# Gated feed-forward up-projection: seven-product pairs raised from 8 to 14 per layer, weight sums formed by adding transfers in memory

## The chip, the cores and the metric

The kernel runs on one core of a Trainium2 chip. The metric is the device time of one execution in microseconds; a run's time is the median over repeated executions. The profile shown here is of one execution on the same core. The engines are called PE (TensorE, with PEld for its weight loads), DVE (VectorE), ACT (ScalarE), POOL (GpSimd) and SP (SyncE, which here only issues transfers).

## The reference

The kernel computes a two-layer decoder trunk on 512 tokens of width 1024, all in float32. Each layer has an attention mixer and then a gated feed-forward block with a causal convolution of width 3 along the tokens. Only the feed-forward block matters here:

```python
def causal_dwconv(h, w, b):          # w: (3, channels), one filter per channel
    y = lax.conv_general_dilated(h, w[:, None, :], (1,), [(CONV_WIDTH - 1, 0)], ...,
                                 feature_group_count=c)
    return y + b

def conv_ffn(h, w_up, conv_w, conv_b, w_down):      # h: (1, 512, 1024)
    u = causal_dwconv(h @ w_up, conv_w, conv_b)     # w_up: (1024, 5632)
    gate, up = jnp.split(u, 2, axis=-1)             # 2816 each
    return (jax.nn.silu(gate) * up) @ w_down        # w_down: (2816, 1024)

for i in range(DEPTH):                              # DEPTH = 2
    ...                                             # mixer, residual
    h = conv_ffn(rms_norm(x, ffn_pre_g[i]), ffn_w_up[i], ffn_conv_w[i], ffn_conv_b[i], ffn_w_down[i])
    x = x + rms_norm(h, ffn_post_g[i])
```

## The kernel before, in words

**Numbers in two parts.** Every float32 operand of a large product is split into a high and a low part (`split`, `Weights.split`: ACT rounds the high part, DVE subtracts it from the value). A product is three matmuls, high by high, high by low and low by high (`mm3`, lines 290 to 292). A weight *unit* is a 128x1024 float32 block: SP loads it into one of three buffers `wraw` (line 52 or 144), ACT makes `wh` (line 74), DVE makes `wl` (line 75). The class `Weights` keeps a list of units, in the order of use, and prepares some of them ahead of the product that uses them.

**The up-projection.** 2816 gate and 2816 up features are 22 blocks of 128 each. A *pair* is one gate block and the up block that multiplies it; there are 22 pairs, indexed by `n`. The input is held transposed, features of the model on the partitions (8 blocks `k` of 128) and the 512 tokens along the row. An ordinary pair takes 2 (gate, up) x 8 (`k`) x 3 = 48 matmuls of 512 tokens. After it, ACT scales the sum out of PSUM (line 509), DVE adds the two shifted taps (lines 510 and 512), ACT applies silu (line 514), and DVE multiplies gate by up. After each second pair DVE also forms four sums and differences of token blocks (lines 529 to 532) and splits one block of results (`split`, line 199), because the down-projection is done with seven products too.

**Seven products.** For the pairs in `SEVEN` (8 of 22) the product is seen as two by two blocks: gate or up, by the lower or upper half of `k`, by the lower or upper half of the tokens. Seven block products take the place of eight (Strassen's scheme in Winograd's form). One block product is 4 (`k`) x 3 = 12 matmuls of 256 tokens, so a pair takes 84 of these. Four of the seven use sums of input blocks (`x_sums`, made once per layer), and four use sums of weight blocks. In the kernel before, the weight sums are made by `up_sums`: it loads the same two units that an ordinary pair loads and lets DVE do four 128x512 additions or subtractions (lines 150, 151, 154 and 157) on the raw blocks before the split. A seven-product pair has 3.5 units to split (three of 1024 columns and one of 512), an ordinary pair two. Between the products ACT copies two 256-wide partial results (lines 468 and 472) and DVE adds one of them to PSUM twice (lines 475 and 479).

**What sets the order.** In the up-projection of the kernel before, a planner that knows the instructions' estimated costs sets the order on each engine; it may mix the matmuls of an ordinary pair among those of a seven-product pair. In other stages the order is written out by hand (`manual_schedule`). Each engine's queue runs strictly in its order, whoever set it. SP's queue holds nearly all loads. POOL's queue holds small 128x1 operations: the reciprocal roots of the norms in attention (up to 36 us and again from 140 us in layer 0) and at the end of each feed-forward block; in between it is empty.

Of the kernel before, what the change touches and what calls it, by code (L numbers as in the profile page):

```python
# [17 lines left out]
P = 128  # L18
# [18 lines left out]
SEVEN = (4, 6, 8, 10, 12, 14, 16, 18)  # L37


class Weights:  # L40
# [8 lines left out]
    def load(self):  # L49
        src, w = self.units[len(self.raws)]  # L50
        raw = self.raw_pool.tile([P, 1024], F32, tag="wraw", name="wraw", bufs=3)
        self.nc.sync.dma_start(raw[:, :w], src)
        self.raws.append(raw)
# [35 lines left out]
def trunk(tc, A, out):  # L89
# [3 lines left out]
    with ExitStack() as top:  # L93
# [40 lines left out]
        def up_sums(src):  # L134


            raws = []
            lo, hi = slice(0, S), slice(S, 2 * S)

            def unit(n):  # L140
                if n == 0:
                    for z in range(2):
                        raws.append(wpool.tile([P, 1024], F32, tag="wraw", name="wraw", bufs=3))
                        nc.sync.dma_start(raws[z][:], src[z])
                a, b = raws
                h, l = W.pair()
                if n == 0:
                    W.split(h, l, a, 1024)
                elif n == 1:
                    DVE.tensor_tensor(a[:, lo], a[:, lo], b[:, lo], ALU.subtract)  # L150
                    DVE.tensor_tensor(b[:, lo], b[:, lo], b[:, hi], ALU.add)
                    W.split(h, l, b, 1024)
                elif n == 2:
                    DVE.tensor_tensor(b[:, hi], b[:, hi], a[:, lo], ALU.subtract)
                    W.split(h, l, b[:, hi], S)
                else:
                    DVE.tensor_tensor(a[:, hi], a[:, hi], b[:, hi], ALU.subtract)
                    W.split(h, l, a, 1024)
                return h, l

            return [lambda n=n: unit(n) for n in range(4)]

        def ffn_units(layer):
            up = []
            for f in range(NF):
                if f in SEVEN:
                    up += up_sums(A["ffn_w_up"][layer, f])
                else:
                    up += [(A["ffn_w_up"][layer, f, z], 1024) for z in range(2)]
# [203 lines left out]
        def ffn(layer, xnT, pending, final):  # L373
            with ExitStack() as es:
# [3 lines left out]
                nc.sync.dma_start(cw[:], A["ffn_conv"][layer])  # L378
                g_tile = lambda: (fp.tile([P, 1024], F32R, tag="gh", name="gh", bufs=HF),
# [50 lines left out]
                def x_sums():  # L430
# [12 lines left out]

                    def parts(n, x):
# [3 lines left out]
                    return ([lambda: whole_block(a, 0, 0), lambda: whole_block(b, 0, 256), lambda: sub(a, b, a)]  # L448
                            + parts(0, a)
                            + [lambda: whole_block(c, 4, 256), lambda: sub(b, c, b)] + parts(2, b)  # L450
                            + [lambda: sub(c, c, a)] + parts(1, c)
                            + [lambda: whole_block(d, 4, 0), lambda: sub(d, d, c)] + parts(3, d))

                steps = None

                def seven(u, p5):

                    z1, z2 = u[0][:, :256], u[0][:, 256:]
                    c21, c22 = u[1][:, :256], u[1][:, 256:]
                    def product(o, w, half, x, fresh):  # L460
                        for k in range(4):
                            b = slice(half * S + k * P, half * S + (k + 1) * P)
                            xs = [v[:, k] if isinstance(x, list) else v[:, k * 256:(k + 1) * 256] for v in x]
                            mm3(o, w[0][:, b], w[1][:, b], *xs, fresh and k == 0, k == 3, not fresh)

                    wa = W.next()
                    product(c21, wa, 0, x_block(0, 0), True)
                    ACT.copy(z1, c21)
                    wb = W.next()
                    p = bank("t", "p5")[:, :256]  # L470
                    product(p, wb, 0, sums[0], True)
                    ACT.copy(p5, p)
                    wc = W.next()
                    product(c21, wc, 0, sums[1], False)
                    DVE.tensor_tensor(z2, c21, p5, ALU.add)  # L475
                    product(z1, wa, 1, x_block(4, 0), False)
                    wd = W.next()
                    product(c21, wd, 0, sums[2], False)
                    DVE.tensor_tensor(c22, c21, p5, ALU.add)
                    product(z2, wd, 1, x_block(4, 256), False)  # L480
                    product(c21, wb, 1, sums[3], False)

                y1 = None
                for n, f in enumerate(PAIRED):
                    if 3 <= n < min(SEVEN):
                        steps = x_sums() if n == 3 else steps
                        for _ in range(16 if n < min(SEVEN) - 1 else len(steps)):
                            if steps:
                                steps.pop(0)()
                    both = [bank(t, "u") for t in "sa"] if n in SEVEN else None  # L490
                    y = sp.tile([P, 2, S], F32, tag="y", name="y")
# [3 lines left out]
                    if both:  # L495
                        seven(both, y[:, 1, :256])
                    for z in range(2):
                        if n < 2:
                            u = u4[2 * n + z]
                        elif both:  # L500
                            u = both[z]
                        else:
# [233 lines left out]
        def even():  # L736
            with ExitStack() as es:
# [51 lines left out]
                with ExitStack() as e1:  # L789
# [116 lines left out]
                    with ExitStack() as e2:  # L906
# [41 lines left out]
                        for z in range(2):  # L948
                            diff_qk(0, z)
# [840 lines left out]
```

## Time and profile before

| | |
|---|---|
| median of 3 runs | 1136.51 us (1136.33 to 1136.59) |
| profiled execution, its own time | 1136.53 us |
| its span in the trace | 1134.7 us |
| PE busy | 1123.8 us (99%), 6216 matmul records |
| DVE busy | 902.9 us (80%) |
| ACT busy | 614.4 us (54%) |
| POOL busy | 58.2 us (5%) |
| transfers | 126.43 MB, mean 111 GB/s |
| granted PE clock | 0.999 |

The up-projection's matmuls run from 233.8 us to 471.9 us in layer 0 and from 785 us to 1023.5 us in layer 1. The profile's page gives the busy time of each engine and the chain of work that ended last; the views behind it group instructions by line and shape, list them in order of time, say who waited for whom, and give busy time, transfer share and transfer rate for any stretch of the span. A duration in the trace includes some overlap with the next instruction on the same engine, so the distance between two starts is often the better price.

### The profile page before, as it was taken

How to read it: one execution, taken by the hardware profiler on the slowest of the kernel's cores; microseconds unless marked ns; L12 is line 12 of the kernel's file. 1: busy time of each engine (PE TensorE's matmuls, PEld its weight loads, DVE VectorE, ACT ScalarE, POOL GpSimd, SP SyncE). 2: the span in 40 equal slices, each digit the busy share in tenths (PEclk: the TensorE clock that was granted, in tenths of full speed). 3: DMA queues.
4: the chain of work that ended last, by engine and by line, in shares of the span. 5: the costliest groups of instructions: out<-in, count | busy, mean ns of one | idle time of the engine just before them, and what ended most of it. 6: DMA issues, size and time to landing. Idle time of an engine off the chain costs nothing.

```text
span 1134.7 us, 16492 instructions
## 1 busy us (share of the span) xinstructions
PE 1123.8 (99%) x6216; PEld 943.7 (83%) x6216; DVE 902.9 (80%) x1539; ACT 614.4 (54%) x1042; POOL 58.2 (5%) x139
## 2 busy tenths in 40 slices
PE   9999999999999999999999999999999999999997
PEld 8876777898988988887888877888989988988886
DVE  6677576489998998898974476677998998889896
ACT  5465576346555554556643454564455555455562
POOL 2100011210000000000030000002000000000002
PEclk9999999999999999999999999999999999999999
DMA  7310421141423424345736213222123323334461
GB/s 296 112 65 1 137 94 50 44 145 48 144 77 103 119 77 139 107 153 165 228 107 187 88 56 93 77 76 112 59 75 115 109 79 119 101 119 150 146 207 75
DMA packets 39632, 126.43 MB, mean 111 GB/s; under 512 B 5760, under 2 KB 6912, under 8 KB 39424
## 3 DMA queue, kind: packets, MB, share of 16 engines
q1 hardware_dynamic: 37632, 121.63, 33.5%
q10 hardware_dynamic: 1920, 3.74, 1.1%
q8 instruction: 49, 0.80, 0.3%
q14 instruction: 31, 0.25, 0.1%
HBM read 117.98 MB, written 6.32 MB: 110 GB/s over the span
## 4 chain that ended last, share of the span: by engine, by line
PE 89%; DVE 5%; DMA 2%; ACT 2%; issue 2%; POOL 0%; SPq 0%; POOLq 0%; DVEq 0%; ACTq 0%
PE u L290 13%; PE u L292 13%; PE u L291 13%; PE acc L290 4%; PE acc L292 4%; PE acc L291 4%; PE apt L290 3%; PE apt L291 3%; PE apt L292 2%; PE ao L290 2%; PE ao L292 2%; PE ao L291 2%; DVE wl L75 2%; PE sps L984 2%; PE aqk L290 1%
## 5 line engine op out<-in xcount | busy, mean ns | idle before, releaser
L74 ACT CAST wh<-wraw 128x1024 fp32r<-128x1024 f32 (+1 forms) x230 | 232.8, 1019 | 167.0 <-PE u L291 59.2
L75 DVE TENSOR_TENSOR wl<-wraw,wh 128x1024 fp32r<-128x1024 f32 (+1 forms) x230 | 270.4, 1183 | 59.5 <-ACT wh L74 58.9
L290 PE MATMUL u<-xh,wh 128*128 128x512 f32 (+1 forms) x704 | 240.8, 343 | 0.0
L291 PE MATMUL u<-xl,wh 128*128 128x512 f32 (+1 forms) x704 | 240.0, 341 | 0.0
L292 PE MATMUL u<-xh,wl 128*128 128x512 f32 (+1 forms) x704 | 239.5, 341 | 0.0
L290 PEld LDWEIGHTS u<-xh,wh 128*128 128x128 f32 x704 | 133.4, 189 | 17.9 <-DVE u L475 2.6
L291 PEld LDWEIGHTS u<-xl,wh 128*128 128x128 f32 x704 | 133.5, 190 | 14.6
L292 PEld LDWEIGHTS u<-xh,wl 128*128 128x128 f32 x704 | 133.1, 189 | 14.4
L509 ACT ACTIVATE y<-u,cw 128x512 f32<-128x512 f32 x88 | 67.6, 778 | 56.2 <-PE u L292 49.1
L290 PE MATMUL acc<-wh,gh 128*128 128x512 f32 (+1 forms) x250 | 97.0, 388 | 0.8 <-DVE uu L573 0.8
L291 PE MATMUL acc<-wl,gh 128*128 128x512 f32 (+1 forms) x250 | 96.9, 388 | 0.0
L292 PE MATMUL acc<-wh,gl 128*128 128x512 f32 (+1 forms) x250 | 96.9, 387 | 0.0
L510 DVE SCALAR_TENSOR_TENSOR y<-u,cw,y 128x511 f32<-128x511 f32 x88 | 65.0, 744 | 3.1 <-ACT y L509 2.9
L512 DVE SCALAR_TENSOR_TENSOR y<-u,cw,y 128x510 f32<-128x510 f32 x88 | 65.0, 743 | 0.8
L205 POOL TENSOR_TENSOR rv<-ms,epst 128x1 f32<-128x1 f32 x39 | 12.1, 310 | 896.1 <-ACT junk L257 504.6
L290 PEld LDWEIGHTS acc<-wh,gh 128*128 128x128 f32 x250 | 46.9, 188 | 11.0 <-DVE uu L573 1.4
L292 PEld LDWEIGHTS acc<-wh,gl 128*128 128x128 f32 x250 | 46.9, 188 | 9.6
L290 PE MATMUL u<-gh,wh 128*128 128x256 f32 x192 | 54.7, 285 | 0.1
L291 PEld LDWEIGHTS acc<-wl,gh 128*128 128x128 f32 x250 | 47.0, 188 | 9.5
L292 PE MATMUL u<-gh,wl 128*128 128x256 f32 x192 | 54.3, 283 | 0.0
L291 PE MATMUL u<-gl,wh 128*128 128x256 f32 x192 | 54.3, 283 | 0.0
L290 PE MATMUL apt<-xh,wh 128*128 128x512 f32 x128 | 50.6, 395 | 0.0
(360 smaller groups left out, 2317.0 us busy)
## 6 DMA issues: line engine op xcount, KB each, us to landing
wraw<-in_ffn_w_up SPq DMA_DIRECT2D x88, 512.0 KB, 3.7
wraw<-in_ffn_w_down SPq DMA_DIRECT2D x44, 512.0 KB, 3.6
wraw<-in_od_w_dqk SPq DMA_DIRECT2D x12, 512.0 KB, 3.8
wraw<-in_ffn_w_down SPq DMA_DIRECT2D x22, 256.0 KB, 2.9
wraw<-in_ev_w_dqk SPq DMA_DIRECT2D x8, 512.0 KB, 4.5
wraw<-in_ev_w_out SPq DMA_DIRECT2D x8, 512.0 KB, 3.5
spill<-X SPq DMA_DIRECT2D x8, 512.0 KB, 2.6
X<-spill SPq DMA_DIRECT2D x8, 512.0 KB, 6.1
```

The source lines that it names most:

```text
L74: self.nc.scalar.copy(h[:, :w], raw[:, :w])
L75: self.nc.vector.tensor_tensor(l[:, :w], raw[:, :w], h[:, :w].bitcast(F32), ALU.subtract)
L205: POOL.tensor_tensor(v[:, :n], ms, epst[:, :n], ALU.add)
L290: PE.matmul(o, lh, rh, start=first, stop=False, skip_group_check=more)
L291: PE.matmul(o, lh, rl, start=False, stop=False, skip_group_check=more)
L292: PE.matmul(o, ll, rh, start=False, stop=last, skip_group_check=more)
L509: ACT.activation(y[:, z], u, AF.Identity, bias=c[:, 3:4], scale=c[:, 2:3])
L510: DVE.scalar_tensor_tensor(y[:, z, 1:], u[:, :S - 1], c[:, 1:2], y[:, z, 1:], ALU.mult, ALU.add)
L512: DVE.scalar_tensor_tensor(y[:, z, 2:], u[:, :S - 2], c[:, 0:1], y[:, z, 2:], ALU.mult, ALU.add)
L984: PE.matmul(s_ps[:, :w], mq[h][:, i * P:(i + 1) * P], mk[h][:, :w], start=True, stop=True)
```

## The change

`SEVEN` becomes the pairs 4 to 17 of each layer, 14 in place of 8. Six more pairs per layer use seven products, and all seven-product pairs now follow one another.

The weight sums are no longer made by DVE. The host lays the weights of the 14 pairs out as four quarters per pair (`ffn_up_q`: gate lower `k`, gate upper, up lower, up upper). `make_sums` has POOL issue transfers from memory to memory, of which some add to what their destination holds: per pair four sum blocks of 128x512, made in eight steps (four copies, four adds). Three pairs at a time make a *chunk* (`CHUNK = 3`; five chunks, of 3, 3, 3, 3 and 2 pairs), so that one transfer moves 384x512 floats, 768 KB, in rows of 8 KB. Each step waits for the step whose result it uses; the steps of successive chunks overlap by four. Before the steps of a chunk, two one-element transfers from a tile written at a chosen moment (`mark`) keep it from starting sooner. The first two chunks (`EARLY = 2`) of layer 0 are started in the attention of layer 0, those of layer 1 after pair 10 (`OTHER`) of layer 0; the other three chunks start after the first pair (`LATE = 0`) of their own layer.

A unit of a seven-product pair is now two loads of 256 KB (quarters of 128x512, some from `ffn_up_q`, some from the sums `ws`), in the order of use; a pair needs seven quarters, 3.5 units, as before.

In the stretch of the 14 pairs the order on PE, DVE and ACT is written out by hand: the evictions of the last pair are cut into steps and put between the products of the next, the first product of the next pair (`begin_seven`) is put in the middle of the running one, and `more()` prepares one more weight unit at each of seven places per two pairs. Signs change so that fewer kinds of sums are needed: the up half comes out negated, and the taps of those pairs are negated once per layer.

```diff
-SEVEN = (4, 6, 8, 10, 12, 14, 16, 18)
+SEVEN = range(4, 18)
+CHUNK = 3
+EARLY, LATE, OTHER = 2, 0, 10
@@ Weights.load
-        self.nc.sync.dma_start(raw[:, :w], src)
+        if isinstance(src, tuple):
+            for n, part in enumerate(src):
+                self.nc.sync.dma_start(raw[:, n * S:(n + 1) * S], part())
+        else:
+            self.nc.sync.dma_start(raw[:, :w], src)
@@ in place of up_sums
+        def make_sums(layer, chunks, mark):
+            wide = "(a q) c -> a (q c)"
+            tiles = sums_of.get(layer) or [[dpool.tile([CHUNK * P, S], F32, tag=f"ws{layer}{j}{c}", name="ws")
+                                       for c in range(-(-len(SEVEN) // CHUNK))] for j in range(4)]
...
+                nc.gpsimd.dma_start(tiles[j][c][:n].rearrange(wide, q=4), src.rearrange(wide, q=4), accum_op=op,
+                                    max_dma_last_dim=2048)
+            steps = [(0, 3, ALU.bypass), (2, 2, ALU.bypass), (0, 2, ALU.add), (2, 0, ALU.add), (1, None, ALU.bypass),
+                     (1, 0, ALU.add), (3, -1, ALU.bypass), (3, 1, ALU.add)]
+            with tc.manual_schedule(engines={POOL.engine}):
+                for c in chunks:
+                    for j in (0, 2):
+                        nc.gpsimd.dma_start(tiles[j][c][0:1, 0:1], mark)
+                for n in range(len(steps) + 4 * len(chunks)):
+                    for j, c in enumerate(chunks):
+                        if 0 <= n - 4 * j < len(steps):
+                            move(c, *steps[n - 4 * j])
+        def up_blocks(layer):
...
+            parts = [lambda i=i, j=j: block(i, j)
+                     for i, j in ([(0, 0)] + [(i + (j == 0), j) for i in range(len(SEVEN))
+                                              for j in (4, 1, 5, 0, 6, 7, 3)]) if i < len(SEVEN)]
+            return [(tuple(parts[n:n + 2]), S * len(parts[n:n + 2])) for n in range(0, len(parts), 2)]
@@ ffn
+                minus = cw[:, SEVEN[0]:SEVEN[-1] + 1, 1, 0:3]
+                DVE.tensor_scalar(minus, minus, -1.0, None, ALU.mult)
...
+                def seven(n, last):
...
+                    scale, conv, silu, rest = last
+                    heavy = len(rest) > 1
+                    conv(0)
+                    more()
+                    scale(1)
+                    p = bank("t", "p5")[:, :256]
+                    product(p, sums[0], True)
+                    ACT.copy(p5, p)
+                    silu()
+                    if n == OTHER and not final:
+                        ACT.copy(lead[0:1, 1:2], p5[0:1, 0:1])
+                        make_sums(1, range(EARLY), lead[0:1, 1:2])
+                    if heavy:
+                        conv(1)
+                    else:
+                        more()
+                    product(z1, x_block(4, 0), False)
+                    product(c21, sums[1], False)
+                    DVE.tensor_tensor(z2, c21, p5, ALU.add)
+                    if heavy:
+                        rest[0]()
+                    else:
+                        conv(1)
+                    more()
+                    if n != SEVEN[-1]:
+                        begin_seven()
+                    if heavy:
+                        rest[1]()
+                    product(c21, sums[2], False)
+                    DVE.tensor_tensor(c22, c21, p5, ALU.add)
+                    rest[2 if heavy else 0]()
+                    product(z2, x_block(4, 256), False)
+                    more()
+                    product(c21, sums[3], False)
+                    if heavy and n < 2 * (HF - 4) + 2:
+                        rest[3]()
...
+                    if n == SEVEN[0]:
+                        depth, W.depth = W.depth, 0
+                        ready, stop = W.pos + 3, W.pos + (7 * len(SEVEN) + 1) // 2 + 2
+                        W.ahead(ready)
+                        written = tc.manual_schedule(engines={PE.engine, DVE.engine, ACT.engine})
+                        written.__enter__()
+                        begin_seven()
...
+                    if n == LATE:
+                        mark = lead[0:1, 2 + layer:3 + layer]
+                        ACT.copy(mark, y[0:1, 0, 0:1])
+                        make_sums(layer, range(EARLY, -(-len(SEVEN) // CHUNK)), mark)
@@ even, after the norms of the compressed keys
+                        make_sums(0, range(EARLY), rk[0:1, 0:1])
@@ layout
+    q = r["ffn_w_up"][:, SEVEN[0]:SEVEN[-1] + 1].reshape(2, len(SEVEN), 2, P, 2, S)
+    r["ffn_up_q"] = q.transpose(0, 2, 4, 1, 3, 5).reshape(2, 4, len(SEVEN) * P, S)
```

More of the change, by code (lines that the diff above doesn't have):

```diff
@@ L133, in trunk @@
         load_x(3)
[L134 to L155, printed above, removed]
-                else:
[L157 to L161, printed above, removed]
+        sums_of = {}
```

193 lines of the change are left out of this document (122 added, 71 removed).

## The prediction

> **What bounds the kernel now.** I read the page's busy times first, then its chain of waits, then the windows of the up-projection.
>
> ```profile
> PE 1123.8 (99%) x6216; PEld 943.7 (83%) x6216; DVE 902.9 (80%) x1539; ACT 614.4 (54%) x1042; POOL 58.2 (5%) x139
> ```
>
> ```profile
> PE 89%; DVE 5%; DMA 2%; ACT 2%; issue 2%; POOL 0%; SPq 0%; POOLq 0%; DVEq 0%; ACTq 0%
> ```
>
> ```profile
> 281.00:320.00 39.00, 38.93 (x250) 35.19 (x249) 37.08 (x55) 22.69 (x30) 0.00 (x0) 1.00 0.37 108
> 320.00:360.00 40.00, 40.00 (x256) 36.02 (x255) 36.15 (x52) 21.46 (x28) 0.00 (x0) 1.00 0.32 106
> ```
>
> A window row gives its bounds, its length, the busy time of PE, PEld, DVE, ACT and POOL, the granted clock, the transfer engines' share and GB/s. PE never rests: 38.93 of 39 us and 40.00 of 40 us. DVE is close behind (36.15 of 40, 90%), ACT has room, transfers use a third. So what PE saves in the up-projection shows in the total, if DVE and the transfers keep up. What a matmul costs in this stream is the distance between starts:
>
> ```profile
> 295.23 0.40 PE L292 MATMUL u<-xh,wl 128*128 128x512 f32 x1
> ...
> 302.06 0.39 PE L292 MATMUL u<-xh,wl 128*128 128x512 f32 x1
> 302.29 0.28 PE L290 MATMUL u<-xh,wh 128*128 128x256 f32 x1
> ...
> 306.48 0.28 PE L292 MATMUL u<-gh,wl 128*128 128x256 f32 x1
> ```
>
> From 295.23 to 302.29 us there are 31 matmuls of 512 tokens: 7.06 / 31 = 0.2277 us each. The first and last of 36 matmuls of 256 tokens start at 302.29 and 306.48 us: 4.19 / 35 = 0.1197 us. Two narrow ones cost 5% more than one wide one.
>
> **PE's part.** An ordinary pair costs 48 x 0.2277 = 10.93 us, a seven-product pair 84 x 0.1197 = 10.05 us (a product of 12: 1.44 us). The change removes 12 ordinary pairs over the two layers (576 wide matmuls, 131.2 us) and adds 12 others (1008 narrow ones, 120.7 us): **-10.5 us**, all on the path.
>
> **DVE.** Grouped by shape:
>
> ```profile
> L75 DVE TENSOR_TENSOR wl<-wraw,wh 128x1024 fp32r<-128x1024 f32 x214 | 259.4, 1220 | 59.5 <-ACT wh L74 58.9
> L150 DVE TENSOR_TENSOR wraw<-wraw 128x512 f32<-128x512 f32 x16 | 10.9, 681 | 0.0
> L475 DVE TENSOR_TENSOR u<-u,y 128x256 f32<-128x256 f32 x16 | 6.9, 429 | 2.0 <-PE u L292 1.3
> ```
>
> The weight sums leave (four lines like L150: -43.6 us). Each further pair brings 1.5 splits and two 256-wide additions: 12 x (1.5 x 1.22 + 2 x 0.43) = +32.3 us. In total DVE falls by 11 us, but it is now judged on a stretch in which every pair needs 3.5 splits. Spacing of starts, in order of time:
>
> ```profile
> 283.87 0.74 DVE L510 SCALAR_TENSOR_TENSOR y<-u,cw,y 128x511 f32<-128x511 f32 x1
> 284.53 1.21 DVE L75 TENSOR_TENSOR wl<-wraw,wh 128x1024 fp32r<-128x1024 f32 x1
> 285.67 0.74 DVE L512 SCALAR_TENSOR_TENSOR y<-u,cw,y 128x510 f32<-128x510 f32 x1
> 286.32 0.42 DVE L475 TENSOR_TENSOR u<-u,y 128x256 f32<-128x256 f32 x1
> 286.66 0.68 DVE L524 TENSOR_TENSOR hold<-y 128x512 f32<-128x512 f32 x1
> 287.26 1.21 DVE L75 TENSOR_TENSOR wl<-wraw,wh 128x1024 fp32r<-128x1024 f32 x1
> ```
>
> So a split takes 1.14, a tap 0.66, an addition 0.34, a 512-wide product 0.60 us. Per pair: 3.5 x 1.14 + 4 x 0.66 + 2 x 0.34, and per two pairs 2 x 0.60 + 4 x 0.34 + 1.14 for gating and token sums, so 7.31 + 1.85 = 9.16 us under 10.05 us of PE. DVE hides, with 9% to spare. By full durations it would be about 10.2, and DVE would bind by some 0.15 us a pair, 4 us in all; the window row, 90% busy where this spacing gives 88%, speaks for the spacing. The negation of the taps is two small instructions, hidden in the same slack.
>
> **ACT.**
>
> ```profile
> L74 ACT CAST wh<-wraw 128x1024 fp32r<-128x1024 f32 x214 | 223.0, 1049 | 153.1 <-PE u L291 59.2 <-PE apt L291 17.8 <-issue 14.5
> ```
>
> ```profile
> L468 ACT COPY u<-u 128x256 f32<-128x256 f32 x16 | 5.8, 364 | 0.0
> ```
>
> 18 more casts at 1.05 us and 24 more copies at 0.36 us are +28 us over some 280 us, on an engine that is 21.46 of 40 us busy in the window. Hidden.
>
> **After the stretch** come four ordinary pairs in a row. Each leaves DVE 10.93 - (2 x 1.14 + 2.64 + 1.85) = 4.2 us to prepare down-projection weights, where before a seven-product pair stood among the last four. The chain of waits of layer 0 runs through DVE and such loads here:
>
> ```profile
> 466.73 4.76 DMA wraw<-in_ffn_w_down
> ...
> 473.00 0.60 DVE wraw L329
> ```
>
> yet PE loses under 1 us to it (0.77 of 54 us, the window below), so more lead is worth at most that; I count 0, and if the lead shrinks instead, those rows are what comes first.
>
> ```profile
> 480.00:534.00 54.00, 53.23 (x235) 43.59 (x234) 49.31 (x63) 31.70 (x42) 0.00 (x0) 1.00 0.48 155
> ```
>
> **The written order.** Before, the planner could fill a wait with another pair's matmuls; now PE can't. Waits of PE's weight loads on these pairs' additions and copies, 281 to 461 us:
>
> ```profile
> PEld u L290 <- DVE u L475: 1.3, 4, 0.3
> PEld u L290 <- ACT u L468: 0.5, 1, 0.5
> PEld u L290 <- DVE u L479: 0.3, 1, 0.3
> ```
>
> 2.1 us for eight pairs, 0.26 each. Charged in full to 28 pairs that is 7.4 us; the other end is zero, because the order puts the next pair's first product (1.44 us) behind the product that the first addition reads, and another product (1.44 us) behind the one that the second reads. I take a third: **+2.5 us**.
>
> **Loads.** A pair loads seven quarters, 1.835 MB, in 10.05 us: 183 GB/s. What the engines can move, and what one load takes:
>
> ```profile
> 10.00:14.00 4.00, 3.80 (x18) 2.62 (x17) 3.58 (x6) 2.88 (x5) 0.75 (x2) 1.00 1.03 419
> ```
>
> ```profile
> wraw<-in_ffn_w_up SPq DMA_DIRECT2D x88, 512.0 KB, 3.7
> wraw<-in_ffn_w_down SPq DMA_DIRECT2D x22, 256.0 KB, 2.9
> ```
>
> The ceiling is 419 GB/s, so loads take 44% of it. Two sizes give 0.8 us per 256 KB (328 GB/s) on a fixed 2.1 us. A unit is used every 10.05 / 3.5 = 2.87 us; three buffers give a cycle of 8.6 us, less the split on ACT and DVE (2.2 us): a load may take 6.4 us against 3.7. Hidden. SP issues 136 more transfers, about 0.33 us each by the row
>
> ```profile
> 235.88 0.33 SPq L52 DMA_DIRECT2D wraw<-in_ffn_w_up  x1
> ```
>
> or 0.66 us per unit of 2.87: hidden. But its queue is strict: behind a load that waits for a sum stand all later loads, w_down's too.
>
> **The sums.** No row shows a transfer from memory to memory, or one that adds. Lower bound: a plain load at the ceiling, 2.1 + 0.79 MB / 419 GB/s = 4.0 us per 768 KB. Upper bound: an add moves double (it reads its destination too) at 328 GB/s, 2.1 + 4.8 = 6.9 us. I take the lower, nearest to the ceiling row, where many transfers were in flight as here. Late chunks start after pair 0's gating, the row at 263.81 below, plus a copy and the two mark transfers: about 267 us. Pair 4 starts at 280.78:
>
> ```profile
> 263.81 0.69 DVE L517 TENSOR_TENSOR y<-y 128x512 f32<-128x512 f32 x1 [0.19 <-ACT y L514]
> ```
>
> ```profile
> 280.78 0.28 PE L290 MATMUL u<-xh,wh 128*128 128x256 f32 x1
> ```
>
> Pair 10, the first of chunk three, starts six pairs later at 341.1; its last sum is used five products on (348.3), prepared 2.5 units ahead (7.2 us) and loaded (3.7) and cast (1.05) before: **due at 336 us**. The chunk is six dependent slots of at most two transfers: 2.1 + 2 x 1.9 = 5.9 us alone; beside loads that take 44% the transfer part stretches by 1.8, to 8.9 us. Six slots end at 267 + 53 = 320: 16 us early. The next chunk's four further slots take about 7.8 us each, 31 us per three pairs (30.2 us): it keeps pace. Price **0**; if that cover goes, PE waits us for us.
>
> POOL's queue is held while a step waits. Its neighbours:
>
> ```profile
> 35.66 0.55 POOL L208 TENSOR_TENSOR rr<-rv,mhalf 128x1 f32<-128x1 f32 x1
> 96.01 0.10 POOL L1074 MEMSET epsp<- 128x1 f32 x1 [59.80 <-PE sps L984]
> 139.77 0.19 POOL L1135 TENSOR_TENSOR st<-st,epsp 128x1 f32<-128x1 f32 x1 [43.67 <-ACT jk L1133]
> 242.16 0.10 POOL L103 MEMSET spacer<- 128x1 f32 x1
> 566.85 0.64 POOL L205 TENSOR_TENSOR rv<-ms,epst 128x1 f32<-128x1 f32 x1 [324.59 <-ACT junk L257]
> ```
>
> Layer 0's early sums come behind 36 us: nine waits before the last issue, at the upper bound 9 x 2.1 + 53 us of moving, over by about 110. The next that matters is the norm at 139.77, so 30 us of cover; past it, differential attention is late us for us. From 267 us on POOL issues layer 0's late and layer 1's early steps, done by 530 us even at the upper bound; the norms need it at 566.85.
>
> **Sum.** 1136.5 (the profiled execution's own 1136.53, span 1134.7; the median is 1136.51) - 10.5 + 2.5 = **1128.5 us**. PE stays the bound.
>
> **Rivals.** *A, the adds are slow and the sums late: slower.* With adds doubled at 328 GB/s chunk three moves for 43.2 us in its six slots, stretched by 1.8 plus 12.6: 90 us, so 357, 21 us late. At 419 GB/s it is work alone that counts: 52 us of sums and 39 us of loads up to chunk four, 359 against its due 366: not late. A late load frees the engines, so part of a delay is won back: 0 to 21 us per layer, 12 as the middle: 1128.5 + 24 = 1152. It beats the gain from 5 us of lateness per layer. For it: no row shows an add. The Trainium skill, "Collectives: The Full Stack", section "The bandwidth ceiling: the fold count and why AG ≠ RS ≠ AR", says that a transfer that adds runs at half a copy's rate, because it reads two sources; no run here shows it yet, and by it the adds are the doubled ones of this rival.
>
> *B, the sums are in time but crowd out the loads: slower.* Rows of the sums are 8 KB, rows of the loads now 2 KB. If an engine alternates row by row, a load gets a fifth of it: 0.524 MB / 84 GB/s + 2.1 = 8.4 us against the 6.4 allowed, 0.7 us late per unit. Over some 65 units beside moving sums that is 45 us; with equal shares a load takes 4.6 us and costs nothing. Middle: 1128.5 + 22 = 1151. The Trainium skill, "DMA: Bandwidth & Descriptors", section "Queues, rings and completion order", says that each engine goes round its queues packet by packet; the trace of before, with one busy queue, can't show it.
>
> *C, the strict order eats the gain: no change.* The full 7.4 us of waits and DVE bound by 4 us: 1128.5 + 4.9 + 4 = 1137.
>
> **How the numbers follow.** Forecast 0.50, A 0.28, B 0.13, C 0.09. What this kernel's measurement can tell from no change is 0.2%, 2.3 us. Faster: the forecast, 0.02 of A at its lower end and 0.03 of C: 0.55. Same: 0.02 of A, 0.04 of C: 0.06. Slower: 0.39. The likeliest case alone runs from 1125.5 (no waits) to 1133.5 (all of them). The range runs from 1125 to 1162, which leaves out the upper ends of A and B, some 0.15 together.
>
> **What would show it.** PE's narrow matmuls spaced by 0.12 us through the 14 pairs, about 141 us per layer; 768 KB transfers on POOL's queue landing after 4 to 7 us; no idle DVE or ACT before L81's splits on `ws`. Wrong if POOL's adds take over 10 us, if ACT waits on transfers of `ws` or `ffn_up_q` from pair 10 on (A) or from pair 4 on (B), or if PE waits on the two additions in most pairs (C).

## The result, and the profile after

The changed kernel takes **1186.26 us** (median of 4 runs, 1183.08 to 1192.83) against 1136.55 us before: ratio 1.0444, 95% interval 1.0393 to 1.0496. It is slower by 4.4%; the forecast was 1128.5 us. The profiled execution took 1183.08 us, with a span of 1181.3.

Busy times, the chain of waits by engine, the transfer queues (packets, MB, share of 16 engines' span) and some transfers (size in KB, median us to landing), from the page of the changed kernel:

```profile
PE 1126.6 (95%) x6648; PEld 965.9 (82%) x6648; DVE 895.6 (76%) x1511; ACT 633.6 (54%) x1079; POOL 132.5 (11%) x239
...
q1 hardware_dynamic: 57792, 143.66, 36.1%
q0 software_dynamic: 23424, 58.73, 22.2%
...
PE 62%; issue 16%; DMA 11%; DVE 6%; POOL 3%; ACT 2%; SPq 0%; POOLq 0%; DVEq 0%; ACTq 0%
...
ws<-in_ffn_up_q POOLq DMA_DIRECT2D x48, 768.0 KB, 8.0
wraw<-ws SPq DMA_DIRECT2D x112, 256.0 KB, 4.9
...
wraw<-in_ffn_up_q SPq DMA_DIRECT2D x84, 256.0 KB, 5.1
```

PE is busy 95% of the time, where it was 99%. DVE has fallen, as worked out. The chain now runs 11% through transfers (2% before) and 16% through "issue" (2% before), for the most part POOL standing between two sums. A 256 KB load lands after about 5 us; before, one of that size took 2.9 us and one of 512 KB 3.7 us.

The same stretches of layer 0 as in the prediction (bounds, length, busy time of PE, PEld, DVE, ACT and POOL, granted clock, transfer share, GB/s):

```profile
281.00:320.00 39.00, 36.27 (x277) 35.95 (x276) 30.75 (x45) 20.84 (x29) 4.38 (x6) 0.91 0.93 258
320.00:360.00 40.00, 39.24 (x323) 38.66 (x322) 33.88 (x49) 23.43 (x34) 5.08 (x6) 1.00 0.97 272
360.00:400.00 40.00, 28.87 (x224) 28.29 (x223) 25.20 (x34) 17.86 (x25) 4.54 (x6) 0.91 0.88 236
400.00:440.00 40.00, 39.57 (x314) 39.26 (x315) 35.14 (x51) 24.48 (x35) 7.66 (x11) 0.96 0.93 267
480.00:534.00 54.00, 50.76 (x217) 41.41 (x216) 44.52 (x60) 26.55 (x33) 4.12 (x5) 0.97 0.79 213
```

The transfer engines, a third busy before, are now nearly full beside the up-projection: 0.88 to 0.97. PE loses 11 of 40 us in the third stretch and some in each other one, and even the down-projection (last row), dense before, has gaps.

To see which stage pays, the span is cut at the first matmul that writes `u` and the first that writes `acc` (down-projection) in each layer. "Middle" is the down-projection of layer 0 with the attention of layer 1. The kernels in the lower rows are explained below.

| us | attention 0 | up 0 | middle | up 1 | end | span |
|---|---|---|---|---|---|---|
| before | 233.8 | 238.1 | 313.3 | 238.1 | 111.4 | 1134.7 |
| the change | 234.6 | 256.5 | 321.4 | 256.7 | 112.2 | 1181.3 |
| no sums | 234.6 | 232.5 | 311.7 | 232.0 | 111.8 | 1122.7 |
| copies in place of adds | 236.3 | 251.1 | 311.8 | 240.9 | 112.1 | 1152.2 |
| sums that nobody reads | 236.2 | 244.8 | 326.5 | 245.5 | 112.1 | 1165.0 |
| the same, half the rows | 233.4 | 243.0 | 312.1 | 239.5 | 112.2 | 1140.3 |
| the same, runs of 8 KB | 233.9 | 283.2 | 311.8 | 255.5 | 112.3 | 1196.8 |
| the same, runs of 1 KB | 264.4 | 240.3 | 373.2 | 234.6 | 113.4 | 1225.9 |
| layer 1's sums in attention | 234.9 | 256.7 | 356.3 | 235.2 | 111.8 | 1194.9 |
| 6 and 8 pairs | 235.9 | 238.4 | 312.5 | 236.7 | 111.8 | 1135.3 |

Each up-projection pays 18.5 us and the middle 8. A row is one execution; between executions the total of the change varied by 10 us, that of the kernel whose sums nobody reads by 14.

### The profile page after: what moved, and what is told of

The parts are those of the page before. It is cut to its first block, busy times and chain, and to the rows that moved or that the text cites. A ratio compares the mean times of both kernels' runs of the same rounds, so it can differ in the third digit from the quotient of the medians.

```text
span 1181.3 us, 17835 instructions
## 1 busy us (share of the span) xinstructions
PE 1126.6 (95%) x6648; PEld 965.9 (82%) x6648; DVE 895.6 (76%) x1511; ACT 633.6 (54%) x1079; POOL 132.5 (11%) x239
## 3 DMA queue, kind: packets, MB, share of 16 engines
q0 software_dynamic: 23424, 58.73, 22.2%
## 4 chain that ended last, share of the span: by engine, by line
PE 62%; issue 16%; DMA 11%; DVE 6%; POOL 3%; ACT 2%; SPq 0%; POOLq 0%; DVEq 0%; ACTq 0%
PE u L312 4%; PE u L313 4%; PE u L314 4%; PE acc L313 4%; PE acc L312 4%; PE acc L314 4%; DMA wraw<-in_ffn_w_down 3%; PE apt L312 2%; PE apt L313 2%; PE apt L314 2%; DMA wraw<-ws 2%; DMA ws<-in_ffn_up_q 2%; DVE wl L81 2%; DMA ws<-ws 2%; PE ao L312 2%
## 5 line engine op out<-in xcount | busy, mean ns | idle before, releaser
L80 ACT CAST wh<-wraw 128x1024 fp32r<-128x1024 f32 x240 | 249.4, 1047 | 234.8 <-DMA wraw<-ws 64.3
L81 DVE TENSOR_TENSOR wl<-wraw,wh 128x1024 fp32r<-128x1024 f32 x240 | 291.0, 1220 | 99.5 <-ACT wh L80 98.9
L314 PE MATMUL u<-xh,wl 128*128 128x256 f32 (+1 forms) x656 | 206.8, 315 | 0.3 <-DVE wl L81 0.3
L312 PE MATMUL u<-xh,wh 128*128 128x256 f32 (+1 forms) x656 | 207.1, 316 | 0.0
L313 PE MATMUL u<-xl,wh 128*128 128x256 f32 (+1 forms) x656 | 206.9, 315 | 0.0
L312 PE MATMUL u<-gh,wh 128*128 128x256 f32 x336 | 99.8, 297 | 36.9 <-DVE u L584 34.6
L312 PEld LDWEIGHTS u<-gh,wh 128*128 128x128 f32 x336 | 66.5, 198 | 40.8 <-issue 26.4
L159 POOL DMA_DIRECT2D ws<-in_ffn_up_q x60 | 50.9, 848 | 330.7 <-issue 276.2
L313 PEld LDWEIGHTS u<-gl,wh 128*128 128x128 f32 x336 | 66.8, 199 | 0.1
L314 PEld LDWEIGHTS u<-gh,wl 128*128 128x128 f32 x336 | 66.7, 199 | 0.0
```

What stands on the lines that cost most here:

```text
L80: self.nc.scalar.copy(h[:, :w], raw[:, :w])
L81: self.nc.vector.tensor_tensor(l[:, :w], raw[:, :w], h[:, :w].bitcast(F32), ALU.subtract)
L159: nc.gpsimd.dma_start(tiles[j][c][:n].rearrange(wide, q=4), src.rearrange(wide, q=4), accum_op=op, max_dma_last_dim=2048)
L312: PE.matmul(o, lh, rh, start=first, stop=False, skip_group_check=more)
L313: PE.matmul(o, lh, rl, start=False, stop=False, skip_group_check=more)
L314: PE.matmul(o, ll, rh, start=False, stop=last, skip_group_check=more)
```

## Experiments

The theory to test: PE's saving is real, and the sums take it back in two ways, by being late (rival A) and by crowding out the loads (rival B).

**No sums at all.** `make_sums` does nothing, and where a product wants a sum, a plain quarter is loaded.

```diff
         def make_sums(layer, chunks, mark):
+            return
@@ up_blocks
-                return sums_of[layer][j - 4][i // CHUNK][i % CHUNK * P:(i % CHUNK + 1) * P]
+                return A["ffn_up_q"][layer, j - 4, i * P:(i + 1) * P]
```

> The changed kernel without the sum transfers: none is made, and the loads read a plain quarter where they read a sum (so the weight sums are left out of the computation; the products, splits, loads and the written order are all there). If late sums (rival A) or loads crowded out by sum transfers (rival B) cost the time, this gives the forecast's sum, 1128.5 us (1125 to 1133). If the written order itself makes PE wait (rival C), it stays at 1137 us or above, and PE waits for the two DVE additions in most pairs.

Measured: 1124.10 us, ratio 0.9894 (0.9879 to 0.9909). Two windows and the load, in layer 0:

```profile
320.00:360.00 40.00, 40.00 (x335) 39.87 (x333) 37.22 (x52) 26.32 (x37) 0.00 (x0) 1.00 0.56 183
360.00:400.00 40.00, 40.00 (x334) 40.00 (x334) 37.45 (x53) 26.52 (x36) 0.00 (x0) 1.00 0.58 180
```

```profile
wraw<-in_ffn_up_q SPq DMA_DIRECT2D x86, 256.0 KB, 2.8
```

PE is full, DVE 93 to 94% busy beneath it, and loads move 180 to 183 GB/s, as predicted. The written order, the split of work on DVE and ACT and the doubled number of loads cost nothing that shows. Everything that the change lost comes from the sums: 62 us.

**Sums made, but not read.** The transfers of the change run as they are; the loads read plain quarters (the second half of the edit above). Nothing can then be late.

> All sum transfers are made at the same places, but no load reads them: the loads read plain quarters (the weight sums are left out of the computation). The transfers still share the engines with the loads; no load can wait for a sum. If lateness is the cause (A), the time falls to within 5 us of the run without sums, about 1128 to 1134 us. If crowding is the cause (B), at least half of the loss stays: 1155 us or more. Down-projection of layer 0 beside the early sums of layer 1: up to 8 us may stay in either case.

Measured: 1172.22 us (1166.86 to 1180.43). So 48 of the 62 us (43 to 56 by the spread of its runs) need nobody to wait for a sum. In layer 0, ACT's waits for loads from 281 to 470 us, and the loads of that stretch:

```profile
ACT wh L80 <- DMA wraw<-in_ffn_up_q: 40.0, 24, 5.2
```

```profile
wraw<-in_ffn_up_q SPq DMA_DIRECT2D x86, 256.0 KB, 5.4
ws<-in_ffn_up_q POOLq DMA_DIRECT2D x18, 768.0 KB, 8.1
```

Loads that took 2.8 us take 5.4. The changed kernel shows the same on its early sums, which had all been made by about 142 us: ACT waits for a load of them, and soon after PE waits for DVE, whose splits come after these casts.

```profile
305.09 1.05 ACT L80 CAST wh<-wraw 128x1024 fp32r<-128x1024 f32 x1 [5.69 <-DMA wraw<-ws]
```

```profile
311.81 0.58 PE L312 MATMUL u<-gh,wh 128*128 128x256 f32 x1 [2.73 <-DVE u L584]
```

By the table, crowding costs 12.3 and 13.5 us in the two up-projections and 14.8 us in the middle; reading the sums then adds 11.7 and 11.2 us to the up-projections, while the middle loses 5.1 us less.

**Copies in place of adds.** Every step waits and writes as before, but none adds: what the second read is worth.

```diff
-                ... accum_op=op,
+                ... accum_op=ALU.bypass,
```

> The adding transfers become plain copies of the same size at the same places, with the same waits of loads and steps (so the sums are left out of the computation). A copy of 768 KB landed in 4.6 us in a quiet stretch of the changed kernel, an add in 6.9 us. If the double reading of the adds makes the chain late, each of its slots shortens by some 2 to 3 us, the third chunk is ready about 15 us and the fifth about 35 us sooner, and the time falls to 1128 to 1145 us. If the fixed part of each dependent step and the count of steps make it late, little changes: 1170 us or more.

Measured: 1156.03 us, between the two expectations: reading the destination as well is worth some 30 of the 62 us. With copies POOL also stands for "issue" less between two sums (39.7 us from 281 to 470 us, 146.8 in the change), so the 30 us include that. The queue row of POOL's transfers in this kernel (the change's, above, has 22.2% for the same 58.73 MB):

```profile
q0 software_dynamic: 16256, 58.73, 14.2%
```

**Half the bytes.** As the unread kernel, with half of the rows in each transfer.

```diff
-                n = min(CHUNK, len(SEVEN) - c * CHUNK) * P
+                n = min(CHUNK, len(SEVEN) - c * CHUNK) * P // 2
```

> As the kernel whose sums nobody reads (1172.22 us; the weight sums are left out of the products), but each of POOL's transfers moves half of its rows: as many transfers, waits and marks, half the bytes. If it is the engines' time that the loads lack, the loss of 48 us against the kernel without sums (1124.10) halves with the bytes: 1148 us, 1142 to 1154. If it is the number of transfers, or POOL's waits, that costs, it stays at 1165 us or above. If the loss has a threshold (loads in time as long as the engines have a little room), most of it goes: under 1138 us.

Measured: 1142.36 us. The loss falls from 48 to 18 us, a little faster than the bytes, with as many transfers and steps. What costs goes with the bytes, and with the number of runs into which they are cut, which halves too; it is not the number of steps.

**Runs of 8 KB and of 1 KB.** As the unread kernel, with POOL's transfers cut into longer or shorter contiguous runs. The change cuts its rows of 8 KB into runs of 2 KB (`max_dma_last_dim=2048`), as long as the rows of the loads; the rows of 8 KB that rival B reckons with move whole only here. The 1 KB kernel also makes each transfer two, of half the rows.

```diff
-                                    max_dma_last_dim=2048)
+                                    max_dma_last_dim=8192)
```

> As the kernel whose sums nobody reads (1172.22 us; the weight sums are left out of the products), but POOL's transfers are cut into runs of 8 KB in place of 2 KB. If the engines are shared run by run, as rival B had it, the loads with their rows of 2 KB now get a fifth of an engine: a 256 KB load, 5.4 us in the up-projection so far, takes 8 us or more, and the time goes to 1200 us or beyond. If the loads lose only because the engines have no time left (share of 0.9 to 1.0 in that stage), the size of the runs is no matter: 1166 to 1180 us and loads of 5 to 5.7 us.

> As the kernel whose sums nobody reads (1172.22 us; the weight sums are left out of the products), but POOL's transfers are cut into runs of 1 KB in place of 2 KB, each as two transfers of half the rows. If the engines share their time run by run, loads of 2 KB rows get more of it than with runs of 2 KB: they land sooner than the 5.4 us there (some 4 us), and the time falls to 1140 to 1162 us. If the 8 KB runs were slow for another reason, the time stays at 1166 us or above.

Measured: 1197.07 us with 8 KB and 1228.38 us with 1 KB. Loads in layer 0's up-projection, 8 KB first (281 to 470 us), then 1 KB (281 to 440 us):

```profile
wraw<-in_ffn_up_q SPq DMA_DIRECT2D x86, 256.0 KB, 6.9
```

```profile
wraw<-in_ffn_up_q SPq DMA_DIRECT2D x94, 256.0 KB, 4.5
```

4.5, 5.4 and 6.9 us with runs of 1, 2 and 8 KB: the longer the runs of the other queue, the longer a load waits, as rival B said, though with 8 KB less than its fifth of an engine would give (8.4). The up-projection of layer 1, where the same three chunks start after the first pair, loses 2.6, 13.5 and 23.5 us against the kernel without sums. The sums themselves move more slowly in short runs, so part of this is a lower rate; no run separates the two. The total of the 1 KB kernel is a miss for another reason, and POOL's queue shows it:

```profile
172.31 0.97 POOL L161 DMA_DIRECT2D ws<-in_ffn_up_q  x1 [4.61 <-issue]
172.91 0.47 POOL L1204 MEMSET epsp<- 128x1 f32 x1
173.47 0.19 POOL L1265 TENSOR_TENSOR st<-st,epsp 128x1 f32<-128x1 f32 x1
```

The last early sum is issued at 172 us, and the norm that ran at 139.77 us before runs behind it: attention 0 ends 30 us late, the middle 61 us. That is the case the prediction named ("past it, differential attention is late us for us"); the change itself missed it by a hair, with its last early sum issued at 135.34 us.

**Layer 1's sums moved into its attention.** Four of its five chunks start after the value projection of layer 1's attention, with a lag of three steps; layer 0 is as in the change.

```diff
-                        make_sums(layer, range(EARLY, -(-len(SEVEN) // CHUNK)), mark)
+                        make_sums(layer, range((EARLY, 4)[layer], -(-len(SEVEN) // CHUNK)), mark)
@@ odd, after the value projection (and no start after pair 10 of layer 0)
+                ACT.copy(lead[0:1, 1:2], st[0:1, 0:1])
+                make_sums(1, range(4), lead[0:1, 1:2], 3)
```

> Layer 1's sums move: chunks one to four are made during layer 1's attention (steps of successive chunks overlap by five in place of four), only the fifth after the first pair; layer 0 as in the changed kernel, but with no early sums of layer 1 beside its later pairs and its down-projection. A and B both expect layer 1's up-projection to fall from 256.5 us to about 234 us and layer 0's down-projection to lose its 8 us: 1186 - 22 - 8 = 1156 us (1150 to 1163). If the written order is the cause (C), layer 1 stays near 256 us and the time near 1178 us. If the sums hold POOL's queue past the norms that end layer 1's attention, some us come back there.

Measured: 1195.96 us, slower than the change. The up-projection of layer 1 is cured (235.2 us for 256.7), the end of the attention before it is not. Windows, then POOL's queue:

```profile
640.00:720.00 80.00, 79.66 (x428) 63.91 (x427) 50.97 (x72) 41.49 (x44) 10.14 (x13) 1.00 0.74 194
720.00:800.00 80.00, 73.34 (x527) 59.66 (x525) 40.85 (x161) 37.26 (x101) 9.89 (x12) 0.99 0.74 185
800.00:840.00 40.00, 4.22 (x14) 3.75 (x15) 6.90 (x9) 4.85 (x10) 7.58 (x15) 0.50 0.63 139
```

```profile
829.32 0.95 POOL L159 DMA_DIRECT2D ws<-in_ffn_up_q  x1 [3.79 <-DMA ws<-ws]
829.94 0.54 POOL L227 TENSOR_TENSOR rv<-ms,epst 128x1 f32<-128x1 f32 x1
```

Beside attention the sums cost PE nothing (79.66 of 80 us) until the norm stands behind them in POOL's queue; then PE does 4.22 us of work in 40.

**Only as many sums as fit into attention.** The written order with 6 seven-product pairs in layer 0 and 8 in layer 1, all sums made in the attention ahead.

```diff
-SEVEN = range(4, 18)
+KINDS = ("MMMMMM", "MMMMMMMM")
+SEVENS = [range(4, 4 + len(kinds)) for kinds in KINDS]
@@ the starts after pair 0 and pair 10 go; in layer 1's attention:
+                make_sums(1, range(-(-KINDS[1].count('M') // CHUNK)), lead[0:1, 1:2])
```

> The change's written order, with 6 seven-product pairs in layer 0 and 8 in layer 1 in place of 14 and 14; all their sums are made in memory in the attention ahead, two chunks and three, none beside an up-projection or a down-projection. Measured without sums, 28 pairs take 1124.1 us; 14 pairs more by ordinary products cost 14 x 0.88 = 12.3 us: 1136.4 us, 1135 to 1138, if crowding and lateness in the feed-forward blocks were all that the sums cost. If sums beside attention cost too, or the sums of layer 1 hold POOL past the norms, 1140 us or more.

Measured: 1137.82 us, ratio 1.0010 (0.9998 to 1.0022): as before the change, and 1.4 us from the 1136.4 that the theory gave. No sum moves beside a feed-forward block, and there is no loss there (first row); beside the sums, in the attention of layer 1 (second row), PE is full too:

```profile
320.00:360.00 40.00, 40.00 (x270) 36.90 (x269) 37.17 (x52) 23.25 (x30) 0.00 (x0) 1.00 0.58 179
...
620.00:660.00 40.00, 40.00 (x232) 34.60 (x230) 20.17 (x26) 17.95 (x19) 4.63 (x6) 1.00 0.79 204
```

**More pairs with sums on an engine.** Four tries to have more pairs by other means. The kernel before with 14 pairs, sums on DVE (`SEVEN = range(4, 18)` and nothing else):

> The kernel before with 14 pairs by seven products (pairs 4 to 17), sums on DVE as before and the planner's order: the alternative that the sums in memory were to avoid. DVE then needs 9.16 + 4 x 0.60 = 11.56 us per pair against PE's 10.05: 1.51 x 28 = 42 us too much, of which the eight ordinary pairs per layer with some 4 us of slack each can take part only where they stand next to the stretch. If DVE binds: 1136 - 10.5 + 20 to 42 = 1146 to 1168 us. If the planner finds the slack, 1126 to 1136 us.

Measured: 1223.76 us, far above both expectations. The kernel before with 23 pairs, the sums of 14 made in memory beside the attentions and those of 9 on DVE:

> The kernel before with the planner's order, and 23 pairs by seven products in place of 16: 6 in layer 0 and 8 in layer 1 with sums made in memory, all of them in the attention ahead (layer 0 as in the change, layer 1 after the value projection of its attention), the other 9 with sums on DVE. No sum moves beside an up-projection. If crowding of the loads there and late sums are all that was wrong with the change, PE's 7 x 0.88 us come out: 1130 us, 1128 to 1134. If sums cost something beside attention too, or if the planner can't keep DVE (94% busy by the sum of its steps) behind PE, 1136 us or more.

```diff
-SEVEN = (4, 6, 8, 10, 12, 14, 16, 18)
+MEMORY = ((4, 6, 8, 10, 12, 14), (4, 6, 8, 10, 12, 14, 16, 18))
+VECTOR = ((5, 7, 11, 13, 16), (5, 9, 13, 17))
...
```

Measured: 1179.73 us. One window of each, from 360 to 400 us:

```profile
360.00:400.00 40.00, 32.39 (x239) 31.18 (x239) 33.87 (x53) 19.94 (x29) 0.00 (x0) 0.91 0.26 80
```

```profile
360.00:400.00 40.00, 34.53 (x257) 33.22 (x257) 31.87 (x49) 19.31 (x29) 0.00 (x0) 0.91 0.26 82
```

Neither DVE (85% and 80%) nor the transfers (26%) are full: with seven-product pairs in a row under the planner, the engines wait for each other (with 23 pairs, from 281 to 461 us, ACT's casts wait 46.7 us for PE, and DVE's splits 26.9 us for ACT). The planner's order is the likelier reason for both misses, but that is not shown: no run has the same pairs in the written order, and with 14 pairs DVE's own work, 11.56 us a pair by the expectation, exceeds PE's. The written order without sums has no such gaps, so the other two use it: the 6 and 8 pairs, and 3 and 4 more whose quarters DVE adds, or 7 and 6 more whose quarters POOL adds.

```diff
+                else:
+                    nc.sync.dma_start(dst, quarter(i, 3 if j == 4 else 0))
+                    DVE.tensor_tensor(dst, dst, raws[i, 4] if j == 5 else raws[i, "t"][:], ALU.add)
...
@@ the other kernel
-                    DVE.tensor_tensor(...
+                    POOL.tensor_tensor(...
...
```

> As the kernel with 6 and 8 pairs, and 3 and 4 more pairs whose sums DVE makes, put among the others in the written order (9 pairs in layer 0, 12 in layer 1, 21 in all against 16 before). By PE 1124.1 + 7 x 0.88 = 1130.3 us. DVE needs 9.16 us for a pair with sums in memory and 9.16 + 4 x 0.60 = 11.56 for one of its own: 9.96 on the mean against PE's 10.05, so it may bind in places: 1129 to 1135 us. If DVE's additions put the weights late (PE waiting for DVE on the splits), 1137 us or more.

> The change's written order with 13 seven-product pairs in layer 0 and 14 in layer 1. The sums of 6 and 8 of them are made in memory in the attention ahead, as in the kernel with 6 and 8 pairs; for the 7 and 6 pairs between them POOL itself adds the quarters in SBUF, four additions of 128x512 per such pair, where DVE did it in the kernel with 9 and 12. No row shows POOL adding 128x512. One such pair comes every 20.1 us of PE's work, so POOL has 5.0 us for an addition by its total, and some 2 us where an addition stands between a load and its split (three buffers, 8.6 us: 3 for the load, 2.2 for the split). If POOL takes up to 2 us: 1124.1 + 0.9 = 1125 us, 1123 to 1130. If it takes 3 us or more, or makes DVE's instructions longer while it runs, ACT waits for POOL on the splits and the time is 1140 us or more.

Measured: 1147.14 us with DVE (ratio 1.0085, 1.0071 to 1.0099) and 1148.37 us with POOL (1.0089, 1.0074 to 1.0103), both 0.9% above the kernel before. With DVE, its busy time in the stretch is at the limit, and PE misses about a twentieth:

```profile
320.00:340.00 20.00, 19.11 (x157) 18.76 (x157) 19.86 (x29) 12.33 (x17) 0.00 (x0) 1.00 0.55 173
```

With POOL, an addition of 128x512 took 1.4 to 1.8 us on the mean of a group, within the 2 us allowed, yet ACT waited 21.2 us for these additions from 281 to 440 us, and a DVE product of two 128x512 operands (L534) took 1327 ns in that stretch, where it took 686 in the kernel with 6 and 8 pairs. One of POOL's groups in the POOL kernel, then that DVE group from 280 to 430 us, first there, then with 6 and 8 pairs:

```profile
L200 POOL TENSOR_TENSOR wraw<-wraw,tq 128x512 f32<-128x512 f32 x26 | 40.1, 1541 | 225.1 <-DMA wraw<-in_ffn_up_q 150.2 <-DVE y L524 55.8 <-DVE xsum L501 14.7
```

```profile
L534 DVE TENSOR_TENSOR y<-y 128x512 f32<-128x512 f32 x7 | 9.3, 1327 | 0.0
```

```profile
L534 DVE TENSOR_TENSOR y<-y 128x512 f32<-128x512 f32 x7 | 4.8, 686 | 0.1
```

No version tried that forms all its weight sums beats the kernel before.

## Why the prediction was wrong

Two terms that the prediction set at nothing cost the time: the sums ("Price **0**") and the loads ("Hidden"). Of the 62 us, 48 stay when nobody reads the sums, which is loads crowded out; reading the sums adds the other 14.

**PE's part: right.** -10.5 us was worked out; the kernel without sums gains 5.6 and 6.1 us in its two up-projections, 11.7 in all.

**The written order: too dear.** +2.5 us was charged; no window without sums shows a gap. Rival C falls. The two kernels with pairs in a row under the planner, with some or all of their sums on DVE, are worse by far (1223.76 and 1179.73 us).

**DVE, ACT, the ordinary pairs after the stretch: right**, hidden.

**The sums: the step that failed first.** "I take the lower" set 4.0 us for every transfer of 768 KB. Two of the change's early transfers, with little beside them, the copy issued at 113.00 us and the add at 135.34 us, landed after

```profile
ws<-ws POOLq DMA_DIRECT2D x1, 768.0 KB, 4.6
```

```profile
ws<-in_ffn_up_q POOLq DMA_DIRECT2D x1, 768.0 KB, 6.9
```

The add is the upper bound to the tenth. The Trainium skill, "Collectives: The Full Stack", section "The bandwidth ceiling: the fold count and why AG ≠ RS ≠ AR", puts a collective that reduces at half the rate of one that copies, because its add reads two sources. The two durations (a ratio of 1.5 with the fixed part in both) agree in direction. So do the two queue rows, by an estimate: with copies alone the queue's time is 14.2% of 1152.2 us, 164 us, so half of the steps as copies take 82 us, and in the change the other half, as adds, take 262 - 82 = 180 us, 2.2 times as much. The kernel with copies puts 30 us on it. The add stood in rival A and should have stood in the sum.

Nor were there six slots. POOL mostly issued one step at a time and stood idle 7 to 8 us between ("issue"), although the step it was to issue next had no unfinished input that the profile names:

```profile
269.87 1.29 POOL L159 DMA_DIRECT2D ws<-in_ffn_up_q  x2
278.31 1.01 POOL L159 DMA_DIRECT2D ws<-in_ffn_up_q  x1 [7.16 <-issue]
...
331.59 0.98 POOL L159 DMA_DIRECT2D ws<-in_ffn_up_q  x1 [7.49 <-issue]
...
381.56 0.96 POOL L159 DMA_DIRECT2D ws<-in_ffn_up_q  x1 [7.16 <-issue]
```

Chunk three's last add is issued at 331.59 us and lands 8 us on, at about 340 where 320 was forecast and 336 due. Its eight steps took eight slots: seven of them from 269.87 to 331.59 us, 8.8 us each, as long as the 8.9 us forecast for a slot of two. In the kernel with runs of 8 KB, where POOL does not stand like this, the same add is issued at 305.08 us, in the sixth slot. Chunk four's last add, issued at 381.56 and landed at 389.3, is 23 us behind its due time of 366. One wait shows the whole path, add, load, cast, split, addition (the chain of waits, then PE):

```profile
381.56 7.76 DMA ws<-in_ffn_up_q
...
390.17 7.15 DMA wraw<-ws
...
397.40 1.05 ACT wh L80
398.45 0.02 issue
398.48 1.23 DVE wl L81
399.70 0.35 DVE u L584
```

```profile
400.19 0.55 PE L312 MATMUL u<-gh,wh 128*128 128x256 f32 x1 [8.88 <-DVE u L584]
...
403.10 0.41 PE L313 MATMUL u<-xl,wh 128*128 128x256 f32 x1
403.31 0.31 PE L314 MATMUL u<-xh,wl 128*128 128x256 f32 x1
403.46 0.28 PE L312 MATMUL u<-xh,wh 128*128 128x256 f32 x1
403.58 0.28 PE L313 MATMUL u<-xl,wh 128*128 128x256 f32 x1
```

The change less the unread kernel is 11.7 and 11.2 us in the up-projections: rival A's middle was 12 per layer. That it fits so closely is luck: 12 was the middle of 0 to 21 us, rival A had chunk three 21 us late where it was 4, and the two totals vary by 10 and 14 us.

**Loads: the step that cost most.** "A load may take 6.4 us against 3.7. Hidden" compared the allowance with a load that has the engines to itself. Beside the sums the median is 4.9 to 5.4 us, still under 6.4, yet ACT waited 24 times for a load in one up-projection of the unread kernel, up to 5.2 us: the median hides the late ones (the load on the chain above took 7.15). Rival B put 22 us on this; the unread kernel shows 25.8 in the two up-projections and 14.8 in the middle, which B did not count. B had the right step, but its size is luck: it reckoned with 8 KB rows against 2 KB rows, and with equal shares, which the change's runs of 2 KB come nearer to, it gave a load 4.6 us and no cost. The middle pays only where sums still move when the down-projection begins: the last early sum of layer 1 is issued at 517 us in the unread kernel and at 514 in the change, but by 444 us with copies, with half the rows and with runs of 8 KB, and there the middle takes 311.8 to 312.1 us, as without sums. (SP issues 140 more transfers by the page's counts, not 136; that changes nothing.)

**A and B were no alternatives.** They were given 0.28 and 0.13 as rivals; both happened, on the same engines. POOL's queue took 22.2% of the span of 1181.3 us, 262 us of full engine time, or 9.4 us for each of the 28 pairs (the forecast's 1.9 us of moving per 768 KB comes to 5.1; the kernel with 6 and 8 pairs, whose sums have only attention beside them, has 9.3). The late chunks' eight pairs bring 75 us, and loads take 0.57 of the 141 us of the stretch (windows without sums), 80 us: by this estimate 155 us of work for the 155 us from 267 us to the end of the stretch, with nothing left for unevenness. The prediction did add the two demands once, in rival A (52 us of sums and 39 of loads up to chunk four), and found room; with the measured 9.4 us a pair and 0.57 for the loads there is none. Its range ended at 1162: it holds each rival alone at its middle (1152 and 1151), not the two together.

**POOL's cover: right, by less than said.** Layer 0's early sums were to end by 110 us; the last was issued at 135.34, and the norm behind it ran at 140.59 us (139.77 before). The kernels with 1 KB runs and with layer 1's sums in attention show what lies past that edge.

## What to carry to other kernels

Before work is moved onto the transfer engines, add up their engine time in the stage where it will run, an adding transfer counted at the rate of one that reads twice, and compare with the stage's length; a share of a third before says nothing about room for a second stream of the same size. Ask also what stands behind each waiting transfer in its issuing queue. Idle transfer time in another stage can be nearly free (2 and 3 chunks beside the attentions cost 1.4 us by the sum above), so place such work there, and only as much as ends before the queue is next needed.

## What was not expected of the hardware

After a wait of 8.88 us PE ran at about half rate for a while: starts 0.21 us apart from 400.19 to 403.46 us, then 0.12. After the wait of 2.73 us that ended at 311.81 us it did so for 6.2 us. The granted clock of 0.91 in two of the windows above is this, counted over the waits too: it is 1.00 from 393 to 395 us, inside the wait of 8.88, 0.50 from 397 to 399, and 0.51 from 400.1 to 403.4. So a part of what both A and B cost was a price on each gap beside the gap itself: in layer 0 the change's up-projection is 24.0 us longer than without sums, and PE's waits in it come to 16.1 us. The Trainium skill, "TensorE: Matmul & The Clock Gate", section "Part 1: The HAM clock gate (the "warmup" mystery)", says that an array that was idle starts at half its clock for some 3.4 us of work; the 3.3 us after the long wait agree, the 6.2 us after the short one are more.

What holds POOL 7 to 8 us between two transfers is open. From 281 to 470 us "issue" held POOL's sums for 146.8 us in the change and 154.8 us in the unread kernel, whose transfers of 768 KB have 384 runs. With half the rows, 192 runs, it was 8.7 us, and with runs of 8 KB, 96 of them, nothing: POOL was held by transfers instead. So it goes with the number of runs in a transfer; no kernel here shows more.

DVE's two-operand instructions took up to twice their time while POOL added (1327 against 686 ns), which nothing in the trace of before could show. The Trainium skill, "SBUF — State Buffer", section "Terms", describes a port pair that DVE and GpSimd share, held by one of them for a whole instruction while the other waits; these two numbers agree with that.
